# Layer 0's MLP: one convolution and one token-sum part per chunk, a copy moved ahead on ScalarE, weights in four kept tiles

## The chip, the cores and the metric

The kernel runs on one NeuronCore of a Trainium2 chip. A core has TensorE (PE, matrix products, 128 rows by 128 columns of weights), VectorE (DVE), ScalarE (ACT) and GpSimd (POOL) for elementwise work, SyncE (SP), which here only issues DMAs, and DMA engines that move data between device memory and the core's on-chip memory. TensorE writes into PSUM, eight banks of 128 x 512 fp32 numbers; the other operands lie in SBUF. Every engine works through its own instructions in order and waits on semaphores for the others. The metric is the time of one execution on the device, in microseconds (us).

## The reference

Two layers of a decoder over 512 tokens and 1024 channels. Layer 0 mixes tokens by causal means over windows, layer 1 by sliding-window attention; behind each stands a gated MLP with a causal convolution of width 3 over tokens. The change concerns the MLP of layer 0:

```
def rms_norm(x, g):
    y = xf * lax.rsqrt(jnp.mean(xf * xf, axis=-1, keepdims=True) + RMS_EPS)
    return (y * g.astype(jnp.float32)).astype(x.dtype)
...
def conv_glu_ffn(h, w_in, conv_w, conv_b, w_out):      # w_in: 1024 x 5632, w_out: 2816 x 1024
    u = h @ w_in
    c = lax.conv_general_dilated(u, conv_w..., padding=[(CONV_W - 1, 0)], ...) + conv_b
    a, g = c[..., :D_FF], c[..., D_FF:]
    return (a * jax.nn.silu(g)) @ w_out
...
    for i in range(DEPTH):
        hn = rms_norm(h, norm_mix[i])
        h = h + (pool_mixer(hn, ...) if i % 2 == 0 else swa_sink_attention(hn, ...))
        hn = rms_norm(h, norm_ffn[i])
        h = h + conv_glu_ffn(hn, ffn_w_in[i], ffn_conv_w[i], ffn_conv_b[i], ffn_w_out[i])
```

## The kernel before

Activations lie transposed: a tile holds 128 channels by 512 tokens, and `h[0..7]` is the residual. fp32 products are made of three matmuls (`mm3`, L87 to L89): each operand is split into a rounded high part, by a ScalarE copy, and the rest, by a VectorE or GpSimd subtraction, and high·high, low·high and high·low are added in a PSUM bank. So every weight tile costs one DMA, one ScalarE copy (L101 in `weights`, L427 in `own_split`) and one subtraction (L104, L428) before TensorE can read it. `weights` takes its tiles from two rings of four, `wh` and `wl`, 1024 columns each.

The MLP of layer 0 (`mlp_halves`, L359) makes 22 pairs of a value and a gate block, 128 channels each. It has three stages.

**Plain chunks.** The first seven pairs (`PLAIN`) are computed directly, one chunk per block: 14 chunks of 8 `mm3` over 512 tokens, that is 24 matmuls each, into a ring of eight PSUM banks (`chunk`, L529). Their weights are split on GpSimd (`load`, L525). While TensorE works on chunk `at`, a table of letters at L550 says which other work is issued behind it. `1` runs the next convolution job (`late`, L383: VectorE scales the bank in place at L384, ScalarE starts the convolution at L354, VectorE adds two shifted terms that it reads from the bank at L355 and L356, then the gate's Silu at L367 or the product with the gate at L371 and the split at L379 and L380). A bank is free for a later chunk when L356 has read it. `0` and `2` make the first and second part of the token sums of one channel pair (`first_part`, `second_part`, with VectorE work at L411 to L422 and the splits at L402 and L403); they feed the second stage. `f`, `g`, `r`, `a`, `v` and `m` fetch and split that stage's first weights. The scales `n0_rb` of the RMS norm, which all of this needs, are spread by two pairs of small matmuls in the middle of chunk 3 (`norm.spread`, L230 and L233).

**The loop.** For the pairs 7 to 21 a step (L585) computes value and gate together from sums and differences over two halves of the tokens and weights. It has products of 12 matmuls of 256 tokens with the weights R, W, U and Q. W is R plus U (GpSimd, L466 and L467 in `add_weights`, then a split by `own_split`). Into the half bank of the product with R the product with W is added, and between the two ScalarE copies the bank out (`s1`, L595), so the product with W waits for that copy. Between these products `fill` (L576) puts `mm3` of the down projection, from a generator (`down`, L494) over 48 steps: 6 groups of 2 or 4 z tiles by 8 output blocks. A step's weights are fetched by `down_fetch` (into the ring `sq`, two tiles, shared with the squares of the norms) and split by `down_split` into a tile of `wh` and of `wl`. Step i splits for i+1 and fetches for i+2 behind its first `mm3`. `FILL` says how many `mm3` each loop step takes, 120 in all. SyncE issues the DMAs in program order, and a DMA into a buffer that is still read holds up those behind it.

**The tail.** The down projection's remaining 56 `mm3`, the last group with the sums of squares of the next norm (`after`, L204 and L213 on GpSimd). Then the attention layer begins.

## Time and profile before

| | |
|---|---|
| median of 3 executions | 926.76 us (926.74 to 927.59) |
| the profiled execution | 926.93 us |
| its span (first to last instruction) | 925.2 us |
| mean granted TensorE clock | 0.994 |
| plain chunks, loop, tail in that span | about 26 to 111, 111 to 361, 361 to 399 us |

The profile is one execution. Its page gives each engine's busy time; further views of the same trace give the time line of one engine, the waits grouped by who waited for whom, the chain of instructions that ended last, and the busy time of all engines in chosen windows. In a row of the time line stand the start, the duration, the engine, the line of the program, the operation with the tile written and the tiles read, shapes, and in brackets the idle time before it with the instruction that ended it. Matmuls overlap each other, so the spacing of their starts says more than their durations.

### The profile page before, as it was taken

To read this page: it belongs to the slowest core of one execution; us is meant where nothing else is said; L and a number is where in the kernel's file an instruction comes from. 1 tells how busy PE (TensorE), PEld (TensorE's weight loads), DVE (VectorE), ACT (ScalarE), POOL (GpSimd) and SP (SyncE) were. 2 spreads that over 40 slices of the span, in tenths; PEclk is the share of its full clock that TensorE was granted. 3 is DMA by queue.
4 is the path that set the end of the run, shared out by engine and by line. 5 is a ranking of instruction groups with operands and counts; after the bars stand their busy time and mean duration, and the time that the engine had idled before them with its cause. 6 is when DMAs were issued, how large, how long until landed. Compare 5 with 4: busy or idle time off the path is not lost.

```text
span 925.2 us, 13037 instructions
## 1 busy us (share of the span) xinstructions
PE 900.2 (97%) x4812; PEld 772.1 (83%) x4812; DVE 702.9 (76%) x1116; ACT 478.9 (52%) x776; POOL 247.1 (27%) x319
## 2 busy tenths in 40 slices
PE   9998989999999999999999999999999999999996
PEld 8886789988889988779888988888888888888885
DVE  7899978777787886566788572699995888976744
ACT  7754554555555553444878551465343444533434
POOL 3856313113131310153666221000230001200004
PEclk9999999999999999999999999999999999999999
DMA  8435244643655542133211032328177232443302
GB/s 325 145 114 134 83 114 129 178 127 105 169 146 147 141 134 71 55 111 101 77 46 47 1 112 94 115 69 247 49 186 224 92 93 66 92 157 97 110 24 92
DMA packets 37120, 106.85 MB, mean 115 GB/s; under 512 B 3904, under 2 KB 4928, under 8 KB 37056
## 3 DMA queue, kind: packets, MB, share of 16 engines
q1 hardware_dynamic: 33744, 93.95, 30.8%
q0 software_dynamic: 3312, 12.06, 7.6%
q8 instruction: 38, 0.62, 0.3%
q14 instruction: 26, 0.21, 0.1%
HBM read 103.90 MB, written 2.10 MB: 115 GB/s over the span
## 4 chain that ended last, share of the span: by engine, by line
PE 66%; DVE 3%; ACT 2%; DMA 2%; issue 1%; POOL 1%; ACTq 0%; DVEq 0%; SPq 0%; POOLq 0%
PE bank L89 21%; PE bank L87 21%; PE bank L88 21%; PE bank L1102 1%; PE bank L1130 1%; DMA uw_u_raw<-w_half 1%; DMA wo_raw<-w_down 1%; DVE wo_l L104 1%; ACT sc L1118 1%; DVE uw_u_l L428 0%; ACT wo_h L101 0%; PE bank L745 0%; DVE h L505 0%; DVE uw_r_l L104 0%; ACT uw_u_h L427 0%
## 5 line engine op out<-in xcount | busy, mean ns | idle before, releaser
L87 PE MATMUL bank<-f1x_h,wi_h 128*128 128x512 f32 x352 | 137.9, 392 | 0.0
L89 PE MATMUL bank<-f1x_h,wi_l 128*128 128x512 f32 x352 | 137.1, 390 | 0.0
L88 PE MATMUL bank<-f1x_l,wi_h 128*128 128x512 f32 x352 | 137.0, 389 | 0.0
L101 ACT ACTIVATE wi_h<-wi_raw 128x1024 fp32r<-128x1024 f32 x58 | 61.1, 1059 | 86.9 <-PE bank L88 67.9
L104 DVE TENSOR_TENSOR wi_l<-wi_raw,wi_h 128x1024 fp32r<-128x1024 f32 x44 | 53.7, 1225 | 31.8 <-ACT wi_h L101 31.7
L89 PEld LDWEIGHTS bank<-f1x_h,wi_l 128*128 128x128 f32 x352 | 66.1, 188 | 13.9
L88 PEld LDWEIGHTS bank<-f1x_l,wi_h 128*128 128x128 f32 x352 | 66.1, 188 | 13.5
L87 PEld LDWEIGHTS bank<-f1x_h,wi_h 128*128 128x128 f32 x352 | 66.1, 188 | 13.5
L466 POOL TENSOR_TENSOR uw_r_raw<-uw_r_raw,uw_u_raw 128x512 f32<-128x512 f32 x15 | 22.0, 1464 | 179.5 <-DVE uw_r_l L104 173.2
L104 POOL TENSOR_TENSOR wi_l<-wi_raw,wi_h 128x256 fp32r<-128x256 f32 x56 | 53.9, 1044 | 38.4 <-ACT wi_h L101 38.4
L101 ACT ACTIVATE wo_h<-wo_raw 128x512 fp32r<-128x512 f32 (+2 forms) x56 | 36.6, 659 | 42.0 <-PE bank L88 33.9
L87 PE MATMUL bank<-f0x_h,wi_h 128*128 128x512 f32 x112 | 43.9, 398 | 3.5 <-DVE g_t L356 3.5
L634 DVE TENSOR_TENSOR c_u<-bank,n_rb 128x512 f32<-128x512 f32 x44 | 30.1, 687 | 21.8 <-PE bank L89 21.8
L213 POOL TENSOR_TENSOR n_acc<-n_acc,n_sq 128x512 f32<-128x512 f32 x14 | 21.1, 1506 | 90.4 <-ACT n_sq L204 90.3
L88 PE MATMUL bank<-f0x_l,wi_h 128*128 128x512 f32 x112 | 44.3, 396 | 0.0
L89 PE MATMUL bank<-f0x_h,wi_l 128*128 128x512 f32 x112 | 44.2, 394 | 0.0
L505 DVE TENSOR_TENSOR h<-bank,h 128x512 f32<-128x512 f32 x48 | 32.9, 685 | 13.4 <-PE bank L89 13.2
L104 DVE TENSOR_TENSOR wo_l<-wo_raw,wo_h 128x512 fp32r<-128x512 f32 (+2 forms) x52 | 38.0, 731 | 6.6 <-ACT wo_h L101 6.0
L639 DVE SCALAR_TENSOR_TENSOR c_t<-c_u,vec,c_t 128x510 f32<-128x510 f32 x44 | 40.9, 932 | 1.2
L776 POOL TENSOR_TENSOR wt_a_raw<-wt_a_raw,wt_s_raw 128x1024 f32<-128x1024 f32 x4 | 11.3, 2834 | 103.3 <-DVE wt_a_l L104 103.3
L87 PE MATMUL bank<-th,uw_v_h 128*128 128x256 f32 x120 | 34.5, 287 | 4.3 <-ACT sn L595 4.3
L637 ACT ACTIVATE c_t<-c_u,vec 128x512 f32<-128x512 f32 x44 | 35.3, 806 | 2.8 <-DVE c_u L634 2.6
(438 smaller groups left out, 2834.1 us busy)
## 6 DMA issues: line engine op xcount, KB each, us to landing
wi_raw<-w_in SPq DMA_DIRECT2D x58, 512.0 KB, 3.4
wo_raw<-w_down SPq DMA_DIRECT2D x40, 256.0 KB, 3.0
uw_u_raw<-w_half SPq DMA_DIRECT2D x15, 512.0 KB, 3.7
uw_u_raw<-w_half POOLq DMA_DIRECT2D x15, 512.0 KB, 7.2
uw_r_raw<-w_half SPq DMA_DIRECT2D x15, 512.0 KB, 4.6
wt_a_raw<-w_tok SPq DMA_DIRECT2D x12, 512.0 KB, 4.0
kq_raw<-w_kq SPq DMA_DIRECT2D x10, 512.0 KB, 3.4
wo_raw<-w_o SPq DMA_DIRECT2D x8, 512.0 KB, 3.3
```

Source lines behind the costliest of these rows:

```text
L87: T.matmul(ps, lhsT=wh, rhs=xh, start=start, stop=False, **kw)
L88: T.matmul(ps, lhsT=wh, rhs=xl, start=False, stop=False, **kw)
L89: T.matmul(ps, lhsT=wl, rhs=xh, start=False, stop=stop, **kw)
L101: pin(A.activation(h[:, :n], raw[:, :n], AF.Copy))
L104: (eng or V).tensor_tensor(l[:, o], raw[:, o], h[:, o].bitcast(F32), ALU.subtract)
L213: eng.tensor_tensor(self.acc[:, lo:hi], self.acc[:, lo:hi], sq[:, lo:hi], ALU.add)
L466: G.tensor_tensor(r[:, :n], r[:, :n], u[:, n:], ALU.add)
L505: V.tensor_tensor(h[m], ps, h[m], ALU.add)
L634: V.tensor_tensor(u, ps, rb, ALU.mult)
L637: A.activation(t, u, AF.Identity, bias=col(V_CB + layer * 2 * NF + m), scale=cw[2])
L639: V.scalar_tensor_tensor(t[:, 2:], u[:, : S - 2], cw[0], t[:, 2:], ALU.mult, ALU.add)
L776: G.tensor_tensor(r[:, :n], r[:, :n], raws["s1", s][:, :n], ALU.add)
```

## The change

It has three parts.

First, the table of letters: from chunk 3 on each chunk gets one convolution job and one part of the token sums; before, the sums came first in a bunch. The norm's scales are spread two `mm3` later in chunk 3 (k == 7 instead of 5). The weights of one later chunk are loaded a chunk earlier. R's first raw tile comes from another ring.

Second, in a loop step the split of the next step's R and U (`first_weights`, `add_weights`) stands behind the copy `s1`, the rest of the step before and the first fill, no longer ahead of the product with R. Q's split moves behind `last()`.

Third, R, Q and the down projection's weights no longer draw from the rings `wh` and `wl`: these are taken whole, as four pairs of kept tiles (`hold`). Tiles 0 and 2 hold R in turns, tile 1 holds Q and every third down step, tile 3 the two other down steps. Down weights are split two steps ahead and fetched four ahead, with the same two raw buffers. `FILL` and the two banks of the fills change as well.

```diff
@@ -444,20 +444,30 @@
             if j > PLAIN:
                 rs[j] = wp.tile([P, 1024], F32, tag="raw", name=f"uw{j}_r_raw", bufs=3)
             else:
-                rs[j] = fp.tile([P, 1024], F32R, tag="vl", name=f"uw{j}_r_raw", bufs=3).bitcast(F32)
+                rs[j] = fp.tile([P, 1024], F32R, tag="vh", name=f"uw{j}_r_raw", bufs=3).bitcast(F32)
             nc.sync.dma_start(blocks(rs[j]), w_half[j - PLAIN][:, 0:2, :])
 
+        hold, half = [], 4 * P
+
+        def keep():
+            hold.append(tuple(wp.tile([P, 1024], F32R, tag=f"w{k}", name=f"uw_hold{len(hold)}_{k}") for k in "hl"))
+
+        def kept(i, cut, raw):
+
+            w = tuple(t[:, cut] for t in hold[i])
+            A.activation(w[0], raw, AF.Copy)
+            V.tensor_tensor(w[1], raw, w[0].bitcast(F32), ALU.subtract)
+            return w
+
         def first_weights(j):
 
-            n = 4 * P
-            u, r = us[j], rs[j]
             if j > PLAIN:
                 q = wp.tile([P, 1024], F32, tag="raw", name=f"uw{j}_q_raw", bufs=3)
             else:
                 q = sm.tile([P, S], F32, tag="sq", name=f"uw{j}_q_raw")
-            nc.sync.dma_start(q[:, :n], w_half[j - PLAIN][:, 3, :])
+            nc.sync.dma_start(q[:, :half], w_half[j - PLAIN][:, 3, :])
             raws[j] = q
-            uw[j] = weights(None, 2 * n, f"uw{j}_r", raw=r), own_split(u, f"uw{j}_u")
+            uw[j] = kept((j - PLAIN) % 2, slice(0, 1024), rs[j]), own_split(us[j], f"uw{j}_u")
 
         def add_weights(j):
 
@@ -468,7 +478,11 @@
 
         def second_weights(j):
 
-            uw[j] += own_split(rs.pop(j), f"uw{j}_v"), weights(None, 4 * P, f"uw{j}_q", raw=raws.pop(j))
+            uw[j] += (own_split(rs.pop(j), f"uw{j}_v"),)
+
+        def last_weights(j):
+
+            uw[j] += (kept(2, slice(0, half), raws.pop(j)[:, :half]),)
 
         def product(out, w, b, t, start=True):
             for p in range(4):
@@ -488,7 +502,9 @@
         def down_split(i):
             if i < len(steps):
                 g, m = steps[i]
-                w = weights(None, DOWN0[g] * P, f"wo{g}_{m}", raw=down_raw.pop(i))
+                n = DOWN0[g] * P
+                at, a = (2, half) if i % 3 == 0 else (3, i % 3 * half - half)
+                w = kept(at, slice(a, a + n), down_raw.pop(i)[:, :n])
                 down_w[i] = [part(w, k) for k in range(DOWN0[g])]
 
         def down():
@@ -499,8 +515,8 @@
                 for k in range(n):
                     mm3(ps, w[k], z[first + k], k == 0, k == n - 1)
                     if k == 0:
-                        down_split(i + 1)
-                        down_fetch(i + 2)
+                        down_split(i + 2)
+                        down_fetch(i + 4)
                     if k == n - 1:
                         V.tensor_tensor(h[m], ps, h[m], ALU.add)
                         if g == len(DOWN0) - 1:
@@ -537,17 +553,19 @@
         for k in range(NC):
             for i in range(2):
                 mm3(pss[i], part(w[i], k), xs[k], k == 0, k == NC - 1)
-        ahead = load(2)
+        ahead = [load(2)]
         for at in range(2, len(todo)):
-            w, ps, ahead = ahead, chunk(at), load(at + 1)
+            w, ps = ahead.pop(0), chunk(at)
+            for i in {11: (12, 13), 12: ()}.get(at, (at + 1,)):
+                ahead.append(load(i))
             for k in range(NC):
                 if at == 3 and k == 0:
                     r = norm.stats(bank("aux"), root=True)
-                if at == 3 and k == 5:
+                if at == 3 and k == 7:
                     rb = norm.spread(bank("aux"), r)
                     signs = spread_signs()
                 mm3(ps, part(w, k), xs[k], k == 0, k == NC - 1)
-            for x in {3: "00", 4: "00", 5: "1", 6: "22", 7: "12", 8: "21ff", 9: "1g1", 10: "1r", 11: "11", 12: "1av", 13: "g1m1"}.get(at, ""):
+            for x in {3: "01", 4: "01", 5: "01", 6: "01", 7: "21f", 8: "21f", 9: "21", 10: "21g", 11: "1r", 12: "1a", 13: "vgm"}.get(at, ""):
                 if x == "0":
                     first_part(len(th))
                 elif x == "2":
@@ -558,19 +576,24 @@
                     fetch_sums(PLAIN + fetched)
                     fetched += 1
                 elif x == "r":
+                    keep()
+                    keep()
+                    hold.insert(1, None)
                     first_weights(PLAIN)
                 elif x == "g":
                     fetch_rows(PLAIN + (at > 12))
                 elif x == "a":
                     add_weights(PLAIN)
                 elif x == "m":
+                    last_weights(PLAIN)
                     down_fetch(0)
                     down_fetch(1)
                     down_split(0)
+                    down_fetch(2)
                 else:
                     second_weights(PLAIN)
 
-        FILL = dict(zip(range(PLAIN, NF), (11, 11, 10, 9, 8, 8, 7, 7, 7, 7, 7, 7, 7, 7, 7)))
+        FILL = dict(zip(range(PLAIN, NF), (11, 10, 9, 8, 8, 8, 8, 8, 8, 7, 7, 7, 7, 7, 7)))
         fills = down()
 
         def fill(j, i):
@@ -578,15 +601,18 @@
             for x in range(n * (i + 1) // 4 - n * i // 4):
                 next(fills)
 
+        hold.pop(1)
+        keep()
+        keep()
+        hold.insert(1, hold.pop(2))
+        down_split(1)
+        down_fetch(3)
         ring = rings["ps"]
-        rings["aux"] = ring[2:4]
-        rings["ps"] = ring[:2] + ring[4:]
+        rings["aux"] = [ring[1], ring[3]]
+        rings["ps"] = [ring[0], ring[2]] + ring[4:]
         last = None
         for j in range(PLAIN, NF):
-            R, U, W, Q = uw.pop(j)
-            if j + 1 < NF:
-                first_weights(j + 1)
-                add_weights(j + 1)
+            R, U, W = uw[j][:3]
             ba, bx = bank("ps"), bank("ps")
             s1, s2 = (fp.tile([P, HS], F32, tag="sn", name=f"sn{j}{i}", bufs=4) for i in range(2))
             s3 = sm.tile([P, S], F32, tag="sqa", name=f"sn{j}2", bufs=1)[:, lo]
@@ -595,8 +621,13 @@
             A.activation(s1, ba[:, lo], AF.Copy)
             if last:
                 last()
+                last_weights(j)
+            Q = uw.pop(j)[3]
             work()
             fill(j, 0)
+            if j + 1 < NF:
+                first_weights(j + 1)
+                add_weights(j + 1)
             product(ba[:, lo], W, 0, 5, False)
             A.activation(s2, ba[:, lo], AF.Copy, scale=-1.0)
             if j + 1 < NF:
```

On VectorE, in the plain stage, the changed table brings the convolution's reads of bank 4 forward. These are its rows before (the bank of chunk 2, whose gate terms are `g1_t`; `ty`, `tv`, `th`, `tl` are the token sums; numbers behind a name's last underscore only number the tiles):

```order
L384 TENSOR_TENSOR bank4_74<-bank4_74,n0_rb_595 128x512
L422 TENSOR_TENSOR tv3_841<-ty3_667,tv3_841 128x256
L403 TENSOR_TENSOR tl2_659<-tv2_801,th2_658 128x1024
L384 TENSOR_TENSOR bank5_75<-bank5_75,n0_rb_595 128x512
L403 TENSOR_TENSOR tl3_666<-tv3_841,th3_665 128x1024
L355 SCALAR_TENSOR_TENSOR g1_t_849<-bank4_74,vec_90,g1_t_849 128x511
L355 SCALAR_TENSOR_TENSOR a1_t_894<-bank5_75,vec_90,a1_t_894 128x511
L356 SCALAR_TENSOR_TENSOR g1_t_849<-bank4_74,vec_90,g1_t_849 128x510
L356 SCALAR_TENSOR_TENSOR a1_t_894<-bank5_75,vec_90,a1_t_894 128x510
```

And these are the rows now:

```order
L355 SCALAR_TENSOR_TENSOR g1_t_715<-bank4_74,vec_90,g1_t_715 128x511
L380 TENSOR_TENSOR z0l_671<-a0_t_665,z0h_670 128x512
L356 SCALAR_TENSOR_TENSOR g1_t_715<-bank4_74,vec_90,g1_t_715 128x510
L403 TENSOR_TENSOR tl2_708<-ty2_709,th2_707 128x768
L411 SCALAR_TENSOR_TENSOR ty3_755<-h1_97,vec_90,mx_603 128x2x256
L412 SCALAR_TENSOR_TENSOR ty3_755<-h3_99,vec_90,px_604 128x512
L384 TENSOR_TENSOR bank5_75<-bank5_75,n0_rb_601 128x512
L419 TENSOR_TENSOR tv0_803<-ty0_613 128x256
L403 TENSOR_TENSOR tl3_754<-ty3_755,th3_753 128x768
```

Before, the second L356, which frees bank 4, was the 45th VectorE instruction after the first that needs `n0_rb`; now it is the 19th, and the sums of the channel pairs 2 and 3 follow it.

On ScalarE, where the loop begins, these are the rows around the first `s1` (`sn70`) before:

```order
L367 ACTIVATE g5_t_1107<-g5_t_1107 128x512
L354 ACTIVATE a5_t_1141<-bank5_75,vec_90 128x512
L354 ACTIVATE g6_t_1217<-bank0_70,vec_90 128x512
L101 ACTIVATE uw8_r_h_1114<-uw8_r_raw_1086 128x1024
L595 ACTIVATE sn70_1124<-bank6_76 128x256
L379 ACTIVATE z5h_1146<-a5_t_1141 128x512
```

And now:

```order
L458 ACTIVATE uw_hold3_h_1108<-wo0_2_raw_1104 128x512
L367 ACTIVATE g5_t_1131<-g5_t_1131 128x512
L458 ACTIVATE uw_hold2_h_1106<-uw8_r_raw_1094 128x1024
L354 ACTIVATE a5_t_1205<-bank5_75,vec_90 128x512
L621 ACTIVATE sn70_1114<-bank6_76 128x256
L354 ACTIVATE g6_t_1263<-bank0_70,vec_90 128x512
L632 ACTIVATE sn71_1115<-bank6_76 128x256
```

The copy `sn70` now stands ahead of `g6_t` and of the split of pair 8's R, and still behind `a5_t`, which reads bank 5 after VectorE has scaled it.

On SyncE's queue, for one step in the loop, the order before was this (`w_half` are the loads of U, R and Q, `w_down` those of the down projection, with group and block in the tile's name):

```order
L439 DMA uw11_u_raw_1565<-w_half 128x2x512
L486 DMA wo0_6_raw_1444<-w_down0 128x512
L458 DMA uw10_q_raw_1486<-w_half 128x512
L448 DMA uw11_r_raw_1568<-w_half 128x1024
L486 DMA wo0_7_raw_1481<-w_down0 128x512
L486 DMA wo1_0_raw_1589<-w_down1 128x512
L439 DMA uw12_u_raw_1747<-w_half 128x2x512
```

And now:

```order
L439 DMA uw11_u_raw_1534<-w_half 128x2x512
L500 DMA wo1_0_raw_1423<-w_down1 128x512
L468 DMA uw10_q_raw_1507<-w_half 128x512
L448 DMA uw11_r_raw_1537<-w_half 128x1024
L500 DMA wo1_1_raw_1462<-w_down1 128x512
L439 DMA uw12_u_raw_1709<-w_half 128x2x512
L500 DMA wo1_2_raw_1560<-w_down1 128x512
```

The loads of the down projection stand two steps earlier relative to those of U, Q and R.

## The prediction

> **What bounds the kernel now.** I read the page's busy times first, then the busy time in windows, then TensorE's time line where a window has idle, and last the engine that ended the idle.
>
> ```profile
> span 925.2 us, 13037 instructions
> ...
> PE 900.2 (97%) x4812; PEld 772.1 (83%) x4812; DVE 702.9 (76%) x1116; ACT 478.9 (52%) x776; POOL 247.1 (27%) x319
> ...
> core 0: us, PE busy (x) PEld busy (x) DVE busy (x) ACT busy (x) POOL busy (x), PEclk, DMA share, GB/s
> 42.90:50.20 7.30, 6.91 (x35) 5.57 (x36) 4.61 (x9) 1.59 (x3) 6.05 (x9) 1.00 0.45 150
> 50.20:84.20 34.00, 34.00 (x151) 27.89 (x149) 32.31 (x41) 17.17 (x22) 19.81 (x18) 1.00 0.48 128
> 84.20:118.20 34.00, 26.57 (x115) 21.64 (x114) 32.11 (x45) 21.26 (x31) 12.82 (x14) 0.95 0.25 81
> 118.20:200.00 81.80, 81.76 (x536) 75.22 (x537) 63.79 (x86) 42.32 (x65) 20.18 (x15) 0.98 0.49 136
> 200.00:280.00 80.00, 76.02 (x520) 68.59 (x519) 62.45 (x92) 41.30 (x67) 20.23 (x15) 1.00 0.56 149
> ...
> 340.00:361.00 21.00, 20.29 (x137) 18.41 (x136) 14.14 (x23) 9.66 (x16) 0.00 (x0) 1.00 0.35 111
> ...
> 380.00:400.00 20.00, 17.89 (x72) 12.56 (x71) 12.67 (x17) 11.30 (x19) 6.54 (x5) 1.00 0.14 40
> ```
>
> TensorE is busy in 97% of the span, so the change can only win what TensorE idles in layer 0's MLP, and the half clock that follows a long idle. The windows put a limit on that. Idle is 34.00 − 26.57 = 7.43 us where the plain chunks end, 3.98 + 0.71 = 4.69 in the loop after 200, 2.11 in the tail. In the two plain windows VectorE is busy 64.4 of 68 us: there it is the second bound, and the decisive one. The waits name who ended TensorE's idle:
>
> ```profile
> PE bank L89 <- DVE wo_l L104: 5.9, 8, 1.1
> ...
> PE bank L87 <- ACT sn L595: 4.3, 2, 4.0
> ...
> PE bank L87 <- DVE g_t L356: 3.5, 1, 3.5
> ```
>
> **Term A, the plain chunks.** Two idles, each seen on TensorE's time line:
>
> ```profile
> 83.92 0.39 PE L89 MATMUL bank<-f0x_h,wi_l 128*128 128x512 f32 x1
> 87.83 0.66 PE L87 MATMUL bank<-f0x_h,wi_h 128*128 128x512 f32 x1 [3.52 <-DVE g_t L356]
> ...
> 91.28 0.43 PE L89 MATMUL bank<-f0x_h,wi_l 128*128 128x512 f32 x1
> ...
> 113.90 0.39 PE L89 MATMUL bank<-z1h,wo_l 128*128 128x512 f32 x1
> 118.24 0.39 PE L87 MATMUL bank<-th,uw_v_h 128*128 128x256 f32 x1 [3.95 <-ACT sn L595]
> ...
> 118.93 0.42 PE L88 MATMUL bank<-tl,uw_v_h 128*128 128x256 f32 x1
> 119.14 0.41 PE L89 MATMUL bank<-th,uw_v_l 128*128 128x256 f32 x1
> ```
>
> The first: chunk 10 needs bank 4, which L356 of `g1_t` frees. That L356 was the 45th VectorE instruction behind the norm's scales and is now the 19th. 45 took until about 87.8, so 19 should end near 66, and the idle goes. With it goes the half clock: from 87.83 to 91.28 eight matmuls started 0.43 us apart in place of 0.227, 1.6 us. A whole chunk without a wait is 24 x 0.227 = 5.44 us.
>
> But TensorE then runs into the second wait, and that one hangs on VectorE:
>
> ```profile
> 50.25 1.30 DVE L384 TENSOR_TENSOR bank<-bank,n_rb 128x512 f32<-128x512 f32 x2 [1.21 <-ACT n_rb L233]
> ...
> 84.48 1.23 DVE L403 TENSOR_TENSOR tl<-tv,th 128x1024 fp32r<-128x1024 f32 x1 [1.93 <-ACT th L402]
> ...
> 96.99 0.69 DVE L371 TENSOR_TENSOR a_t<-a_t,g_t 128x512 f32<-128x512 f32 x1 [1.36 <-ACT g_t L367]
> ...
> 114.81 1.28 DVE L384 TENSOR_TENSOR bank<-bank,n_rb 128x512 f32<-128x512 f32 x2
> ...
> 115.53 0.78 ACT L354 ACTIVATE a_t<-bank,vec 128x512 f32<-128x512 f32 x1
> 116.20 0.77 ACT L354 ACTIVATE g_t<-bank,vec 128x512 f32<-128x512 f32 x1
> 116.86 1.05 ACT L101 ACTIVATE uw_r_h<-uw_r_raw 128x1024 fp32r<-128x1024 f32 x1
> 117.81 0.38 ACT L595 ACTIVATE sn<-bank 128x256 f32<-128x256 f32 x1
> ```
>
> The `s1` copy at 117.81 stands on ScalarE behind `a5_t` (115.53), which cannot start before VectorE scales its bank (the first half of the pair at 114.81, so about 115.45). Of the three instructions between, the change moves two behind the copy, 116.20 and 116.86: 0.66 + 0.95 = 1.6 us. `a5_t` stays. So the new time is VectorE's. Before, 82 instructions lie between 50.25 and 115.45; 65.2 us, less the idles 1.93 and 1.36, is 61.9. After, the same 82 lie before that point in another order, and two 512-column splits of down weights are new.
>
> ```profile
> 76.25 1.22 DVE L380 TENSOR_TENSOR z0l<-a_t,z0h 128x512 fp32r<-128x512 f32 x1
> ...
> 91.19 0.68 DVE L380 TENSOR_TENSOR z1l<-a_t,z1h 128x512 fp32r<-128x512 f32 x1
> ...
> 74.43 4.49 POOL L104 TENSOR_TENSOR wi_l<-wi_raw,wi_h 128x256 fp32r<-128x256 f32 x4
> ...
> 91.35 1.68 POOL L466 TENSOR_TENSOR uw_r_raw<-uw_r_raw,uw_u_raw 128x512 f32<-128x512 f32 x1 [1.22 <-DVE uw_r_l L104]
> 93.11 1.29 POOL L467 TENSOR_TENSOR uw_r_raw<-uw_r_raw 128x512 f32<-128x512 f32 x1
> ```
>
> A subtraction of that size took 0.68: 1.3 for two, as they start about 0.65 apart. Pair 7's W has R's split, L466, L467 and a ScalarE copy ahead of its own split: 1.68 + 1.29 + about 1.05 (the 1024-column copy at 116.86) = 4.0, and the new order queues some 2.9 us of VectorE work beside it, so 1.1 idle is new. The start moves too: spreading the scales two `mm3` later is 6 x 0.227 = 1.4 us later, of which the wait for the norm's statistics, 0.4 to 0.9 in the first window, falls away; I take 0.5. So VectorE ends at 50.75 + 61.9 + 1.3 + 1.1 = 115.05, `a5_t` starts at 115.15 and `s1` 0.67 behind it, and it takes 0.38: W starts at 116.2 in place of 118.24. **A = −2.0.** Without any wait TensorE would be there at 84.15 + 4 x 5.44 + 1.4 (R) + 1.4 (two fills) = 108.7, so it idles over 7 us at one place where it idled at two; the half clock behind `s1` (119.14 and 118.93 lie 0.21 apart, and the next window's clock is 0.98) stays. Bounds: if VectorE's cover were gone the gain would be 118.24 − 108.7 = 9.5 and, with a short wait, both ramps: 11.9; if its work grew by another 2 us, nothing.
>
> That VectorE's 61.9 us stay is the weak point. The same subtraction took 1.22 beside four GpSimd splits (74.43) and 0.68 without. Free durations for the 82 sum to about 52, so some 9.7 us are contention, and a new order may put other VectorE work beside GpSimd's. Instructions that read a PSUM bank (L355, L356, L384) keep their 0.7 throughout, and six of the eight VectorE instructions of a pair's two convolution jobs are of that kind. GpSimd's splits are the same in number and go on at TensorE's pace. I take no gain, with 9.7 as the end.
>
> The Trainium skill, GPSIMD Engine Reference, section 8. Key points, says that GpSimd shares its SBUF interfaces with VectorE and contends with VectorE instructions with two SBUF inputs. By that rule, the trace agrees: 0.68 against 1.22. It speaks for a gain wherever a convolution's bank reads replace token sums beside GpSimd: up to 9.7 us of A, against the 2.0 of the sum.
>
> **Term B, the loop.** The eight waits of L89 on `wo_l` are a down step's low part, split only one step ahead:
>
> ```profile
> 240.36 0.40 PE L88 MATMUL bank<-z8l,wo_h 128*128 128x512 f32 x1
> 241.89 0.50 PE L89 MATMUL bank<-z8h,wo_l 128*128 128x512 f32 x1 [1.13 <-DVE wo_l L104]
> ```
>
> The starts lie 1.53 apart in place of 0.227, so a wait costs 1.3 where the row says 1.13: 0.17 more. In the loop that is 4.69 idle + 8 x 0.17 = 6.0. With the split two steps ahead, a step of at least two `mm3` (1.4 us) and the products between lie in the gap, more than the longest wait of 1.3. The kept tiles do not stall ScalarE for this: the copy for i+2 overwrites the tile of i−1, whose last reader is already past. Moving `first_weights` behind the first fill puts 2 copies and 2 splits later, but they are for the next step, a good 15 us off. I leave 0.5 as new waits: **B = −5.5**, between −6.0 and +1 (the waits only move).
>
> **Term C, the tail.** Same waits, plus the load of the raw tile: two `sq` buffers are shared with the norm's squares, and each square waits for GpSimd's sum.
>
> ```profile
> 390.14 1.29 POOL L213 TENSOR_TENSOR n_acc<-n_acc,n_sq 128x512 f32<-128x512 f32 x1 [2.57 <-ACT n_sq L204]
> ...
> 394.03 0.63 ACT L101 ACTIVATE wo_h<-wo_raw 128x512 fp32r<-128x512 f32 x1 [1.25 <-DMA wo_raw<-w_down]
> ```
>
> With fetches two steps earlier, the last two loads wait for squares 1 and 2, not 3 and 4, so the 1.25 on the DMA goes. 2.11 idle + 5 x 0.17 = 3.0: **C = −3.0**, between −3.0 and 0.
>
> **The sum.** −2.0 − 5.5 − 3.0 = −10.5, against the profiled execution's 926.93: 916.4 us. That execution lies 0.17 above the median of the runs shown, so the two hardly differ.
>
> **The rivals.**
>
> *Both idles of the plain chunks vanish* (VectorE loses half its contention or more): A from −9.5 to −11.9, total −18 to −20.4, 906.5 to 909. For it: 9.7 us of contention are there. Against: GpSimd's work and VectorE's overlap as before in length. 0.12. The Trainium skill, TensorE: Matmul & The Clock Gate, Part 1, says that after an idle window of about 3.4 us the clock halves until about 3.4 us were busy. By that rule, the trace agrees: 3.52 idle, then 0.43 spacing for 3.5 us. A remaining wait under that length would spare both ramps, which is the 1.6 between the ends here.
>
> *The loop's waits only move*: a deeper fetch changes which semaphore is late, A and C alone: 921.9, up to 924.9 with half of them. 0.13.
>
> *No net effect*: the kept tiles or the later `first_weights` give back what A and C win, within 0.2% (about 1.85 us, roughly what a measurement of this kernel can tell from no change). 0.09.
>
> *Slower, by SyncE's queue.* A down load fetched four ahead must wait for a raw buffer that the split of i+2 frees, which itself waits for TensorE's step i−1. U, Q and R queue behind it. What a late U costs is seen here:
>
> ```profile
> 230.08 7.47 DMA uw_u_raw<-w_half
> ...
> uw_u_raw<-w_half SPq DMA_DIRECT2D x15, 512.0 KB, 3.7
> ...
> SPq L486 <- DVE wo_l L104: 58.2, 38, 4.5
> ```
>
> Instead of 3.7 us it took 7.47, ahead of the wait at 241.89 that cost 1.3. SyncE already waits 58.2 us for `wo_l`, 38 times, mostly unharmed, which speaks against it. If each of the 15 loop steps had such a wait, it would be 15 x 1.3 = 19.5 − 10.5 = +9: 936. It decides from nine of the 15 steps, as 9 x 1.3 = 11.7 is above 10.5. 0.09.
>
> **How the numbers follow.** The forecast has 0.57. The range reaches from 907, inside the case of both idles gone, to 925, the end of that of the moved waits; outside lie the last two cases, 0.18, and a sliver below. Faster by over 0.2%: 0.57 + 0.12 + 0.13 = 0.82; within 0.2% 0.09; slower by over 0.2% 0.09.
>
> **What would show it.** A: no idle near 84, one near 109 of about 7 us ended by `s1`, and VectorE without a gap in between; W at 116. If that idle is under 5 us, VectorE lost contention, and the order's effect on GpSimd's neighbours was my error. B: in the window from 200 to 361 (shifted) under 1 us of idle, and no L89 on a down weight; if ScalarE's `uw_hold` copies wait long for TensorE and L87 waits for them, the kept tiles are the new bound. C: no wait for a DMA in the last group. If TensorE waits for a `w_half` load, the queue decided.

## The result, and the profile after

The changed kernel takes 912.46 us (911.38 to 913.38) against 927.17 us before: ratio 0.9842, 95% interval 0.9823 to 0.9862, 14.7 us faster. One of the four executions before took 1270.42 us; without it the median before is 926.76 us and the gain 14.3 us. 916.4 was forecast, with 907 to 925 as the range: the sign and the places were right, the gain was about a third larger than the 10.5 us of the sum. The profiled execution took 912.77 us, its span 911.1.

The first view is the page of the changed kernel, then busy time in windows of it (window, its length, busy time and count of PE, PEld, DVE, ACT and POOL, granted clock, DMA share, GB/s):

```profile
span 911.1 us, 13018 instructions
...
PE 893.0 (98%) x4812; PEld 773.2 (85%) x4812; DVE 699.4 (77%) x1116; ACT 480.8 (53%) x776; POOL 243.2 (27%) x319
...
50.20:84.20 34.00, 34.00 (x152) 28.14 (x152) 33.25 (x45) 20.26 (x28) 19.94 (x22) 1.00 0.47 131
...
108.60:115.40 6.80, 0.23 (x2) 0.00 (x0) 6.80 (x11) 4.57 (x8) 0.00 (x0) 0.85 0.42 116
115.40:119.40 4.00, 3.96 (x18) 3.96 (x19) 4.00 (x7) 1.04 (x2) 3.22 (x3) 0.50 0.15 41
...
200.00:280.00 80.00, 80.00 (x562) 74.98 (x561) 65.57 (x97) 45.07 (x72) 19.33 (x15) 1.00 0.54 149
...
349.00:369.00 20.00, 20.00 (x90) 16.55 (x89) 13.09 (x22) 6.64 (x11) 0.00 (x0) 1.00 0.32 93
369.00:387.00 18.00, 18.00 (x81) 14.92 (x80) 13.68 (x19) 11.38 (x19) 6.56 (x5) 1.00 0.22 74
```

Loop and tail have no idle left on TensorE. What remains is one long idle where the loop begins (one of 0.36 us lies just ahead of it), with VectorE busy in all of it (6.80 of 6.80), and the half clock behind it (0.50). On TensorE's time line it reads:

```profile
108.44 0.39 PE L89 MATMUL bank<-z1h,uw_hold_l 128*128 128x512 f32 x1
115.44 0.58 PE L87 MATMUL bank<-th,uw_v_h 128*128 128x256 f32 x1 [6.61 <-ACT sn L621]
```

Four starts on TensorE's time line divide the gain: the first product with W, the last product of the loop, the first matmul of attention's `wv` (a little into the next layer, since tail and attention interleave), and the last matmul of the kernel.

| | before | after | gained | forecast |
|---|---|---|---|---|
| A: to the first W | 118.24 | 115.44 | 2.8 | 2.0 |
| B: first W to last product of the loop | 241.11 | 233.18 | 7.9 | 5.5 |
| C: from there to attention's `wv` | 60.42 | 56.31 | 4.1 | 3.0 |
| behind it, with the last instructions | | | −0.7 | 0 |

TensorE's last matmul starts 14.8 us earlier; the span is 14.1 us shorter.

### The profile page after: what moved, and what is told of

Same layout as the page of the kernel before. It is cut to its first block, busy times and chain, and to the rows that moved or that the text cites. A ratio compares the mean times of both kernels' runs of the same rounds, so it can differ in the third digit from the quotient of the medians.

```text
span 911.1 us, 13018 instructions
## 1 busy us (share of the span) xinstructions
PE 893.0 (98%) x4812; PEld 773.2 (85%) x4812; DVE 699.4 (77%) x1116; ACT 480.8 (53%) x776; POOL 243.2 (27%) x319
## 4 chain that ended last, share of the span: by engine, by line
PE 87%; DVE 8%; ACT 3%; issue 1%; POOL 1%; DVEq 0%; ACTq 0%; POOLq 0%
PE bank L87 27%; PE bank L88 27%; PE bank L89 27%; PE bank L1133 1%; PE bank L1161 1%; DVE tl L403 1%; DVE n_acc L531 1%; DVE bank L384 1%; PE bank L285 1%; PE bank L252 1%; ACT sc L1149 1%; ACT h L329 0%; ACT wi_h L101 0%; DVE g_t L356 0%; DVE g_t L355 0%
## 5 line engine op out<-in xcount | busy, mean ns | idle before, releaser
L101 ACT ACTIVATE wi_h<-wi_raw 128x1024 fp32r<-128x1024 f32 x58 | 61.2, 1059 | 87.5 <-PE bank L88 71.2
L104 DVE TENSOR_TENSOR wi_l<-wi_raw,wi_h 128x1024 fp32r<-128x1024 f32 x44 | 53.8, 1225 | 30.5 <-ACT wi_h L101 29.7
L476 POOL TENSOR_TENSOR uw_r_raw<-uw_r_raw,uw_u_raw 128x512 f32<-128x512 f32 x15 | 24.0, 1597 | 162.2 <-DVE uw_hold_l L459 145.4
L89 PE MATMUL bank<-th,uw_hold_l 128*128 128x256 f32 x180 | 51.3, 285 | 0.0
L88 PE MATMUL bank<-tl,uw_hold_h 128*128 128x256 f32 x180 | 51.3, 285 | 0.0
L87 PE MATMUL bank<-th,uw_hold_h 128*128 128x256 f32 x180 | 51.2, 285 | 0.0
```

The source lines that it names most:

```text
L87: T.matmul(ps, lhsT=wh, rhs=xh, start=start, stop=False, **kw)
L88: T.matmul(ps, lhsT=wh, rhs=xl, start=False, stop=False, **kw)
L89: T.matmul(ps, lhsT=wl, rhs=xh, start=False, stop=stop, **kw)
L101: pin(A.activation(h[:, :n], raw[:, :n], AF.Copy))
L104: (eng or V).tensor_tensor(l[:, o], raw[:, o], h[:, o].bitcast(F32), ALU.subtract)
L476: G.tensor_tensor(r[:, :n], r[:, :n], u[:, n:], ALU.add)
```

## The experiments

The first four undo or add one part each. The theory at that point: W waits for VectorE's list, whatever its order; loop and tail gained by the split two steps ahead. The rivals: the early convolutions gained term A, and the kept tiles gained the loop.

**Sums first again.** The table's order of before, less its last convolution job, with the changed loop:

```diff
-{3: "01", 4: "01", 5: "01", 6: "01", 7: "21f", 8: "21f", 9: "21", 10: "21g", 11: "1r", 12: "1a", 13: "vgm"}
+{3: "00", 4: "00", 5: "1", 6: "22", 7: "12", 8: "21ff", 9: "1g1", 10: "1", 11: "11r", 12: "1a", 13: "v1gm"}
```

> The changed kernel with the token sums again ahead of the convolutions in the plain chunks (the same ten jobs before the loop, the same loop). Theory: the product with W waits for VectorE's whole list ahead of the copy s1, and a new order of the same list is worth little. Then the idle near 84 us is back (about 3 us), the one ahead of W is shorter by as much, W starts at 115.4 as in the changed kernel, within 0.8, and the time is 912 to 914 us. Rival: the early convolutions themselves won term A. Then W starts near 118 and the time is 915 to 917.5 us.

Measured: 909.08 us, ratio 0.9804 (0.9788 to 0.9821), 3.4 us faster than the change. Both expectations missed. No idle came back near 84 us, and W started earlier:

```profile
107.45 0.39 PE L89 MATMUL bank<-z1h,uw_hold_l 128*128 128x512 f32 x1
112.52 0.48 PE L87 MATMUL bank<-th,uw_v_h 128*128 128x256 f32 x1 [4.69 <-ACT sn L621]
```

VectorE's time line shows where the difference arises. `z0l` and `z1l` are subtractions of the same size, `tl` one of the token sums. First the changed kernel:

```profile
63.85 1.26 DVE L380 TENSOR_TENSOR z0l<-a_t,z0h 128x512 fp32r<-128x512 f32 x1
...
65.70 3.51 DVE L403 TENSOR_TENSOR tl<-ty,th 128x768 fp32r<-128x768 f32 x1
...
76.94 0.68 DVE L380 TENSOR_TENSOR z1l<-a_t,z1h 128x512 fp32r<-128x512 f32 x1
```

and with the sums first:

```profile
75.38 0.68 DVE L380 TENSOR_TENSOR z0l<-a_t,z0h 128x512 fp32r<-128x512 f32 x1
...
87.79 0.72 DVE L380 TENSOR_TENSOR z1l<-a_t,z1h 128x512 fp32r<-128x512 f32 x1
```

No `tl` of 768 columns took more than 1.5 us with the sums first. From the first scaling by `n0_rb` to the end of the one of bank 5 that `a5_t` waits for, VectorE took 63.3 us in the changed kernel (50.95 to 114.30) and 60.5 here (50.59 to 111.07): for the same 84 instructions it is busy 2.2 us less and idle 0.7 less. So this part of the change costs time. By what, is not shown. Lying beside GpSimd's splits is not enough to be slowed: here one of these splits runs from 73.05 to 78.01 us, beside `z0l`, and it is the split that is long (4.96 us, by the profile's rough span), while `z0l` takes 0.68. Nor do the letters alone decide: in the kernel with the tiles alone (below), which has the sums first too, VectorE was busy 63.2 us with 83 instructions up to the same scaling.

L356 of `g1_t`, which frees bank 4, started at 78.32 us here and at 86.94 in the kernel before, though it is the 41st instruction of the list and was the 45th. So the idle near 84 us goes without the early convolutions. Which of the small differences to the kernel before (the norm's scales, the loads, R's raw tile and split) moved it that far was not taken apart; the tiles alone, with the norm's scales where they were before, left 0.28 us of that idle.

**The next step's splits back at the top of a step.**

```diff
         for j in range(PLAIN, NF):
             R, U, W = uw[j][:3]
+            if j + 1 < NF:
+                first_weights(j + 1)
+                add_weights(j + 1)
...
             fill(j, 0)
-            if j + 1 < NF:
-                first_weights(j + 1)
-                add_weights(j + 1)
```

> The changed kernel with the split of the next step's R and U back at the top of each loop step. Theory: ScalarE's order comes out nearly the same around s1 and the time stays at 912 to 913.5 us. Rival: the later place of these splits is what frees the copies; then s1 waits 1 to 1.6 us longer in the first step and some tenths in others, and the time is 914 to 920 us.

Measured: 912.06 us, ratio 0.9833 (0.9818 to 0.9847): no difference from the change. The order of ScalarE's instructions is set by the program's scheduler, and `sn70` stands ahead of `g6_t` and behind `a5_t` with both placements. The rival falls; the later place of R's and U's splits is worth nothing by itself once the kept tiles are there. Q's split, the other half of the second part, was not moved back.

**One step ahead, tiles kept.**

```diff
-                        down_split(i + 2)
-                        down_fetch(i + 4)
+                        down_split(i + 1)
+                        down_fetch(i + 2)
...
                     down_split(0)
-                    down_fetch(2)
...
-        down_split(1)
-        down_fetch(3)
```

> The changed kernel, kept tiles and all, but down weights split one step ahead and fetched two ahead, as before the change. Theory: the distance of the split is what took TensorE's short waits away. Then L89 waits on the low parts again, loop and tail lose about 8 and 4 us, and the time is 920 to 925 us. Rival: the kept tiles did it, because ScalarE no longer waits for a tile of the rings to come free. Then the time stays within 2 us of the changed kernel, 912 to 915 us.

Measured: 914.91 us, ratio 0.9864 (0.9849 to 0.9878), 2.5 us slower than the change. From the first W to the last product of the loop it takes 233.11 us, as in the change: in the loop the distance gains nothing over the tiles, as the rival said. The loss is all in the tail, 58.96 us in place of 56.31, where the waits for the low part return:

```profile
387.75 0.40 PE L88 MATMUL bank<-ax_l,kq_h 128*128 128x512 f32 x1
388.64 0.50 PE L89 MATMUL bank<-z18h,uw_hold_l 128*128 128x512 f32 x1 [0.50 <-DVE uw_hold_l L459]
```

**Two steps ahead, from the rings.** The kernel before, with

```diff
-                        down_split(i + 1)
-                        down_fetch(i + 2)
+                        down_split(i + 2)
+                        down_fetch(i + 4)
...
                     down_split(0)
+                    down_fetch(2)
...
+        down_split(1)
+        down_fetch(3)
         ring = rings["ps"]
```

> The kernel before with down weights split two steps ahead and fetched four ahead, but from the rings wh and wl as before. If the distance alone does it, loop and tail win 8 and 4 us and the time is 914 to 917 us. If the distance needs the kept tiles, the ring of four runs out: ScalarE's copies wait for TensorE, s1 and the weights behind them are late, and the time is 925 us or more.

Measured: 929.91 us, ratio 1.0026 (1.0016 to 1.0036), the time of the second case. But it is a sum of two things. The tail wins its full 4.1 us (56.31 in place of 60.42). The loop loses 6.4 us (247.55). Its new waits, on TensorE and on ScalarE:

```profile
264.62 0.28 PE L89 MATMUL bank<-th,uw_q_l 128*128 128x256 f32 x1
266.88 0.50 PE L87 MATMUL bank<-z8h,wo_h 128*128 128x512 f32 x1 [1.99 <-ACT wo_h L101]
```

```profile
265.47 1.06 ACT L427 ACTIVATE uw_v_h<-uw_r_raw 128x1024 fp32r<-128x1024 f32 x1 [2.21 <-POOL uw_r_raw L467]
266.43 0.71 ACT L101 ACTIVATE wo_h<-wo_raw 128x256 fp32r<-128x256 f32 x2
```

A down weight that TensorE is already waiting for stands on ScalarE behind the copy of the next W, which waits 2.21 us for GpSimd. That copy is late in most steps. These are the waits over the stretch of the loop, in total, times and the longest:

```profile
PE bank L87 <- DVE bank L618: 5.4, 6, 1.8
```

```profile
ACT uw_v_h L427 <- POOL uw_r_raw L467: 37.8, 13, 4.5
```

Before, the second was 13.2 us in 5 times. Each of the six times, L618 stands on VectorE behind W's split, which waited for that copy. So the second case had the time but not the reason: ScalarE's copies of down weights wait less for TensorE (7.8 us in place of 18.6); W is what comes late. Why GpSimd's sum comes later was not followed. A deeper look-ahead in a ring that R and Q share makes the loop worse.

The next four test the tiles alone and what holds W.

**The tiles alone.** The table with the sums first, the norm's scales at k == 5, the splits at the top of a step, one step ahead, `FILL` and fill banks as before. Q's split stays behind `last()`, and so do R's other raw tile and the earlier load of one chunk's weights. As a diff to the changed kernel, beside the edits of the two experiments on the splits' place and distance:

```diff
-{3: "01", 4: "01", 5: "01", 6: "01", 7: "21f", 8: "21f", 9: "21", 10: "21g", 11: "1r", 12: "1a", 13: "vgm"}
+{3: "00", 4: "00", 5: "1", 6: "22", 7: "12", 8: "21ff", 9: "1g1", 10: "1", 11: "11r", 12: "1a", 13: "v1g1m"}
-                if at == 3 and k == 7:
+                if at == 3 and k == 5:
...
-        FILL = dict(zip(range(PLAIN, NF), (11, 10, 9, 8, 8, 8, 8, 8, 8, 7, 7, 7, 7, 7, 7)))
+        FILL = dict(zip(range(PLAIN, NF), (11, 11, 10, 9, 8, 8, 7, 7, 7, 7, 7, 7, 7, 7, 7)))
...
-        rings["aux"] = [ring[1], ring[3]]
-        rings["ps"] = [ring[0], ring[2]] + ring[4:]
+        rings["aux"] = ring[2:4]
+        rings["ps"] = ring[:2] + ring[4:]
```

> The kernel before with the four kept tiles as the only change: token sums first, R and U split at the top of a step, down weights split one step ahead and fetched two ahead, fills and their banks as before (R's first split stands behind one more job). Theory: the tiles alone end TensorE's waits in the loop. Then from the first W to the last product of the loop it takes 232.5 to 234 us in place of 241.1, the tail keeps 2 to 3 us of waits, and the time is 914 to 921 us, by where W starts. Rival: the loop needs the new banks of the fills, their new spread or the later splits as well; then that stretch takes 236 us or more and the time is 919 us or more.

Measured: 917.87 us, ratio 0.9891 (0.9876 to 0.9906). W starts at 118.34, as before the change; the stretch of the loop takes 233.26 us. The tiles alone win all of term B. In the loop before the change, the copies of down weights wait like this for TensorE to release a tile (total, times, longest):

```profile
ACT wo_h L101 <- PE bank L88: 18.6, 15, 3.8
```

In 13 of the 15 times, 17.0 us, the matmul that ends the wait reads Q or R. One of them, on TensorE and on ScalarE, and the matmul that needs this weight and starts late without any idle in its row:

```profile
148.55 0.28 PE L88 MATMUL bank<-tl,uw_q_h 128*128 128x256 f32 x1
...
148.87 1.27 ACT L101 ACTIVATE wo_h<-wo_raw 128x512 fp32r<-128x512 f32 x2 [2.38 <-PE bank L88]
...
149.55 0.50 PE L87 MATMUL bank<-z0h,wo_h 128*128 128x512 f32 x1
```

With the tiles alone, the same waits of the copies of down weights (`wo_raw`) over the same stretch are (total, times):

```profile
  PE bank L88: 1.2, 5
```

All five end with a matmul of the down projection. The waits for a reader of Q are now those of Q's own copy, 19.6 us in 14 times, and TensorE has no idle from it. So in the ring a down weight takes the oldest tile, also one with R or Q, and waits for its last reader. Whether Q's later split has a share in the gain was not tried apart.

**GpSimd's splits left out.**

```diff
-                return ws0.pop(0) if ws0 else in_weights(0, *todo[i], G)
+                if ws0:
+                    return ws0.pop(0)
+                raw = fetch(w_in[0][todo[i]], D, f"wi{i}")
+                wh = wp.tile([P, 1024], F32R, tag="wh", name=f"wi{i}_h")
+                A.activation(wh, raw, AF.Copy)
+                return wh, wh
```

> The changed kernel without GpSimd's subtractions for plain chunks 4 to 13: the low part of these weights is left out, the matmul reads the high part twice, the count of matmuls stays. Theory: VectorE's list before W is stretched by GpSimd (z0l 1.26 us, z1l 0.68). Then z0l and z2l take 0.68 too, VectorE's list is shorter by 6 us or more, W starts before 110 and the time is 903 to 908 us. Rival: the list is long by its own work; VectorE's durations stay, W starts after 113.5, and the time is 910 us or more.

Measured: 903.2 us, ratio 0.9732 (0.9718 to 0.9746), at the low end of the theory's range. VectorE at the same instructions, and W:

```profile
61.67 0.69 DVE L380 TENSOR_TENSOR z0l<-a_t,z0h 128x512 fp32r<-128x512 f32 x1
...
106.62 1.29 DVE L384 TENSOR_TENSOR bank<-bank,n_rb 128x512 f32<-128x512 f32 x2
```

```profile
107.75 0.39 PE L87 MATMUL bank<-th,uw_v_h 128*128 128x256 f32 x1 [0.24 <-ACT sn L626]
```

The pair of scalings with bank 5 stands at 106.62, at 113.61 in the changed kernel. From the first scaling to that of bank 5, less its idles, the same 84 VectorE instructions take 53.8 us, against 61.1 in the changed kernel: 7.3 us of the list are GpSimd's doing. That is more than the 6.61 us that TensorE idled ahead of W, of which 0.24 is left.

**The first copy first.** The changed kernel, with the copy and the two convolution starts held in program order on ScalarE (`pin`), where the copy comes first:

```diff
-        A.activation(t, ps, AF.Identity, bias=col(V_CB + m), scale=cw[2])
+        c1 = A.activation(t, ps, AF.Identity, bias=col(V_CB + m), scale=cw[2])
+        if m in (5, NF + 5):
+            pin(c1)
...
-            A.activation(s1, ba[:, lo], AF.Copy)
+            c1 = A.activation(s1, ba[:, lo], AF.Copy)
+            if j == PLAIN:
+                pin(c1)
```

> The changed kernel with the first copy s1 held ahead of the convolution starts of pair 5 (L354 of g5_t and a5_t) on ScalarE, nothing else changed by hand. Theory: W waits for VectorE only through a5_t ahead of the copy. Then the copy runs behind z4h and two splits, W starts at 110.5 to 112, and the time is 907.5 to 909.5 us. Rival: W is not what holds TensorE, other VectorE results of the loop are as late; then the idle shows up again within the first loop step, and the time is 911.5 to 913 us.

Measured: 909.91 us, ratio 0.9803 (0.9788 to 0.9818), 2.5 us less than the change, a little short of the theory's 907.5 to 909.5. W starts at 112.40; the loop behind it keeps all but 0.5 of that (233.65 us in place of 233.18). `a5_t` was the gate, but what stands ahead of the copy now is a VectorE result too:

```profile
109.78 0.63 ACT L381 ACTIVATE z4h<-a_t 128x512 fp32r<-128x512 f32 x1 [1.60 <-DVE a_t L373]
110.50 0.63 ACT L460 ACTIVATE uw_hold_h<-wo_raw 128x512 fp32r<-128x512 f32 x1
111.04 1.04 ACT L460 ACTIVATE uw_hold_h<-uw_r_raw 128x1024 fp32r<-128x1024 f32 x1
111.99 0.36 ACT L623 ACTIVATE sn<-bank 128x256 f32<-128x256 f32 x1
```

**Sums first and copy first.** On top of the first experiment, the same hold, and `a4_t`'s job moves into the loop and is held behind the copy as well:

```diff
-... 11: "11r", 12: "1a", 13: "v1gm"}
+... 11: "11r", 12: "1a", 13: "vgm"}
...
+        if m in (4, 5, NF + 5):
+            pin(c1)
```

> Token sums ahead of the convolutions, as in the first experiment, one convolution job fewer before the loop (a4_t goes into it), and the first copy s1 held ahead of a4_t and of pair 5's convolution starts on ScalarE. Theory: nothing of VectorE's convolutions stands ahead of W any more, TensorE runs into the loop with less than 2 us of idle, keeps its clock, and the time is 902.5 to 906 us. Rival: the work that is put off fills VectorE in the first loop steps and TensorE waits there for weights or banks; then the time is 907 us or more.

Measured: 904.97 us, ratio 0.9751 (0.9737 to 0.9765). The idle ahead of W is 1.61 us and the clock stays whole behind it: W's matmuls start 0.12 us apart. One wait of 0.45 us for `sn` stands in the second loop step. What is left ahead of W:

```profile
106.86 1.17 ACT L460 ACTIVATE uw_hold_h<-wo_raw 128x512 fp32r<-128x512 f32 x2 [2.04 <-DMA wo_raw<-w_down]
107.93 1.04 ACT L460 ACTIVATE uw_hold_h<-uw_r_raw 128x1024 fp32r<-128x1024 f32 x1
108.88 0.36 ACT L623 ACTIVATE sn<-bank 128x256 f32<-128x256 f32 x1
```

The last two settle what is left of the order, and of this wait.

**The changed table, copy first.** The same edit on the changed kernel's table (`12: "a"` in place of `12: "1a"`).

> The eighth experiment's edit (one convolution job fewer before the loop, s1 held ahead of a4_t and pair 5's convolution starts) with the changed kernel's own table instead of the sums first. Theory: with s1 free of the convolutions the two orders differ only in how much GpSimd stretches VectorE ahead of pair 7's W; that was 2 to 3 us with the copy behind a5_t, and is still 1 to 3 us: W starts at 110 to 112 and the time is 906 to 908.5 us. Rival: the order of sums and convolutions no longer matters; then the time is within 1 us of the eighth experiment, 904 to 906 us.

Measured: 907.46 us, ratio 0.978 (0.9763 to 0.9797). The time lies where the theory had it, but not by its reason: W starts at 109.91, only 0.6 later than with the sums first. The rest is lost in the second loop step, on another VectorE result:

```profile
125.11 0.28 PE L89 MATMUL bank<-th,uw_hold_l 128*128 128x256 f32 x1
126.61 0.39 PE L87 MATMUL bank<-th,uw_v_h 128*128 128x256 f32 x1 [1.22 <-DVE bank L650]
```

That result, L650's first, is the 96th VectorE instruction of the list in both, 2.3 us later here (126.13 in place of 123.85). VectorE's busy time up to it is nearly the same, 71.2 and 70.8 us; what differs is one idle, 3.62 us in place of 1.61, for ScalarE's copy of pair 7's W. So here the changed table costs a wait for that W, not slower instructions.

**The copy ahead of two splits.** On top of sums and copy first, the splits of `wo0_2` and of pair 8's R are held behind the copy:

```diff
-            A.activation(w[0], raw, AF.Copy)
+            c1 = A.activation(w[0], raw, AF.Copy)
+            if keep_order:
+                pin(c1)
...
-            uw[j] = kept((j - PLAIN) % 2, slice(0, 1024), rs[j]), own_split(us[j], f"uw{j}_u")
+            uw[j] = kept((j - PLAIN) % 2, slice(0, 1024), rs[j], j == PLAIN + 1), own_split(us[j], f"uw{j}_u")
...
-                w = kept(at, slice(a, a + n), down_raw.pop(i)[:, :n])
+                w = kept(at, slice(a, a + n), down_raw.pop(i)[:, :n], i == 2)
```

> The eighth experiment with s1 also held ahead of two more ScalarE copies, the splits of the down weights wo0_2 and of pair 8's R. Theory: the 1.6 us that W still waits are these copies, behind a load that lands late; then W starts within 0.7 us of TensorE's being ready and the time is 903 to 904.3 us. Rival: pair 8's R, split later, makes its W late through GpSimd (a wait of 0.5 us stood there already); then the wait in the second loop step grows by as much as the first shrinks, and the time is 904.5 to 907 us.

Measured: 902.97 us, ratio 0.973 (0.9713 to 0.9747), the best of all, 1.0% below the change. W follows 0.53 us behind the last fill's start, the wait in the second loop step is gone, and no idle is left in loop or tail. The time lies at the low end of the theory's range:

```profile
107.94 0.39 PE L89 MATMUL bank<-z1h,uw_hold_l 128*128 128x512 f32 x1
108.47 0.39 PE L87 MATMUL bank<-th,uw_v_h 128*128 128x256 f32 x1
```

## Why the prediction was right, and where it fell short

All three terms came out larger than forecast. The total lies in the range because its low end, 907, was set by another case, that of both plain idles gone, which did not occur.

**A, forecast 2.0, measured 2.8: the gate was right, the terms were not.** TensorE lost the first idle and ran into one long idle ahead of W, as forecast (6.61 us, "over 7"). VectorE's list and `a5_t` set W:

```profile
112.59 1.04 ACT L458 ACTIVATE uw_hold_h<-uw_r_raw 128x1024 fp32r<-128x1024 f32 x1
114.34 0.78 ACT L354 ACTIVATE a_t<-bank,vec 128x512 f32<-128x512 f32 x1 [0.71 <-DVE bank L384]
115.01 0.37 ACT L621 ACTIVATE sn<-bank 128x256 f32<-128x256 f32 x1
```

Taking `a5_t` from ahead of the copy moved W by 3.0 us. The split of pair 8's R (112.59) has not moved behind the copy, though the prediction and the section on the change say so; it stands ahead of `a5_t`, where ScalarE waits for VectorE anyway. The 1.6 us between `a5_t` and the copy are gone all the same.

The reason given for the first idle, L356 brought from the 45th place to the 19th, was not needed: with the sums first it is the 41st, and the idle is gone too. The list's own time, less idles, was to grow from 61.9 to 63.2 us by two instructions and was 61.1. Pair 7's W made VectorE idle 2.28 us where 1.1 was reckoned; GpSimd took 2.81 and 1.62 us for the two instructions put at 1.68 and 1.29. These two misses pull against each other, so part of A's closeness is luck. The step "I take no gain" from a new order was the weak one, as the text said, but with both signs open: the sums first take 2.9 us less over the same stretch. What GpSimd's splits cost the list is 7.3 us in the changed kernel. The 9.7 of the prediction were for the list before, and an estimate from its rows, against the durations without those splits, gives 9.5. What won the rest of A is not separated: W starts at 118.34 with the tiles alone and at 112.52 with the sums first and the rest of the change.

**B, forecast 5.5, measured 7.9: the size and the reason were off, and the gain lies beyond the term's own bound of 6.0.** The size: the step "In the loop that is 4.69 idle + 8 x 0.17 = 6.0" took only waits that the trace shows as idle. (Nor are these the eight waits of the row: five of those lie in the loop and three in the tail; 0.6 us of the 4.69 are waits for ScalarE's copies.) The busy time of TensorE over the stretch, before and after, from the first W to the loop's last product:

```profile
118.24:359.35 241.11, 236.42 (x1601) 216.81 (x1602) 187.78 (x262) 125.50 (x196) 55.77 (x41) 0.99 0.50 136
```

```profile
115.44:348.62 233.18, 233.18 (x1601) 218.03 (x1602) 188.46 (x263) 127.79 (x196) 52.58 (x41) 0.99 0.52 143
```

The same 1601 matmuls were busy 236.42 and 233.18 us: 3.24 us of the 7.93 gained were never idle. Three rows of the kernel before show such a wait:

```profile
246.40 0.28 PE L89 MATMUL bank<-th,uw_q_l 128*128 128x256 f32 x1
246.66 0.50 PE L87 MATMUL bank<-z8h,wo_h 128*128 128x512 f32 x1
247.00 0.40 PE L88 MATMUL bank<-z8l,wo_h 128*128 128x512 f32 x1
```

They start 0.26 and 0.34 apart where 0.12 and 0.23 are usual: 0.25 us lost, no idle in the row, the second matmul 0.50 long in place of 0.40. Here TensorE waits for ScalarE's copy, the high part, and not for the low part that the term was about. The reason: "With the split two steps ahead, a step ... and the products between lie in the gap" named the distance. In the loop the distance is worth nothing (233.11 us with one step ahead) and is harmful in the rings (247.55). The kept tiles alone give 233.26. What the copies had waited for was a tile shared with R and Q; their place in the program was not too late.

**C, forecast 3.0, measured 4.1: right in its reason, under-sized for the same cause.** It too lies beyond its bound, of 3.0. Here distance counts: 2.7 us of it go with one step ahead, and 4.1 come with two ahead in the rings. The wait for the load, though, did not go. In the changed kernel it reads

```profile
376.77 0.63 ACT L458 ACTIVATE uw_hold_h<-wo_raw 128x512 fp32r<-128x512 f32 x1 [1.34 <-DMA wo_raw<-w_down]
```

and no matmul is late by it.

**The rivals.** Waits that only move: none in the changed kernel (half of A and C would give 924.4 there, not 924.9). Both plain idles gone: not in the change, but reached by the last experiments (the ends of that rival lie 2.4 us apart, not 1.6, as 11.9 less 9.5). SyncE's queue: its waits for down weights grew, and no loop step waited for a load. In the table of the queue's waits before:

```profile
SPq L486 <- DVE wo_l L104: 58.2, 38, 4.5
```

and after:

```profile
SPq L500 <- DVE uw_hold_l L459: 95.8, 35, 6.6
```

So the rival's premise held and its price was nil.

## What to carry to other kernels

A stall shorter than the overlap of two matmuls shows no idle: sum the spacing of starts, or compare busy time for the same count, before a gain is sized. Weights that live for a step and weights that live for a moment should not take turns in one ring; look-ahead helps only when the tile it writes is free. When an engine's list is the bound, look for the one instruction in it that gates the rest, and move that ahead: holding the first copy ahead of the convolutions and putting off one job won 4.1 us on top of the better order.

## What the runs showed of the hardware that was not expected

The half clock behind an idle did not grow with it. Behind 3.31 us (the copy first, with another idle of 1.11 us that ended 4.5 us before) 25 matmul starts were stretched, behind 4.69 us (sums first) 16, behind 6.61 us (the change) 22, and behind 1.61 and 2.00 us (the copy first and one job put off, in either order) none. Nor does contention with GpSimd touch all alike: without its splits the four 768-column subtractions `tl<-ty,th` took 0.96 us on average, with them 1.59; the shifted adds that read a PSUM bank (L355, L356) took 0.74 in both. And it is not always VectorE that is slowed: with the sums first, one split on GpSimd took 4.96 us beside VectorE instructions at their usual durations.
